# Where the lead's second-half shifts, re-roundings and gates stand in ScalarE's queue

## The chip, the cores and the metric

The kernel runs on one core of a Trainium2 chip. The metric is the device time of one execution in microseconds; the time of a kernel is the median of several runs. Beside the times there is one profiled execution, with the start and duration of each instruction on each engine: TensorE (PE, its weight loads PEld), VectorE (DVE), ScalarE (ACT), GpSimd (POOL), and SyncE (SP), which here only issues DMAs.

## The reference

One layer of a streaming encoder over 1024 positions of 1024 channels, in float32:

```python
mod = silu(c) @ w_ada + b_ada
sh1, sc1, g1, sh2, sc2, g2 = split(mod, 6)
h = rms_norm(x, norm_mix_g) * (1.0 + sc1) + sh1
proj = h @ w_in                         # 7 groups of 1024 columns
...                                     # two convolution mixers, sigmoid gates, projections
x = x + g1 * mix
h2 = rms_norm(x, norm_ffn_g) * (1.0 + sc2) + sh2
a, bgate = split(h2 @ w_ffn_in, 2)
x = x + g2 * ((silu(a) * bgate) @ w_ffn_out)
return rms_norm(x, final_norm_g)
```

The change lies in the first part: the making of `h` and the start of `h @ w_in`.

## The kernel before, in words

**Layout.** Everything is kept transposed: channels on the 128 partitions, positions along the row. A block `k` (0 to 7) is 128 channels; a half `h` (0 or 1) is 512 positions. `x[k, h]` is a tile of 128 x 512.

**Precision.** A float32 product is made of three matmuls of a rounded type: each operand is a rounded part `hi` and a rest `lo`, and `mm3` issues hi.hi, hi.lo and lo.hi. So a weight tile that has been loaded (`raw`) is cast on ScalarE (`wh`, L231) and the rest is made by a subtraction on VectorE or GpSimd (`wl`, L232); activations go the same way (`split`, L423; `t_split`, L434 and L435).

**Duals.** Most products with pairs of column blocks are done with a seven-product scheme (Strassen's; the products are named "1265734"). It needs sums and differences of quarter blocks of `h`, in float32: with b11 = `x[k, 0]`, b12 = `x[k, 1]`, b21 = `x[k + 4, 0]`, b22 = `x[k + 4, 1]` the loop at L862 makes b11 - b12, `t2`, b21's difference and, for k = 0, b22 - b12 in place, and splits `t2` for product "6".

**The lead.** While `mod` is still being made, a first stretch of columns (7 blocks of 128, `LEAD`) is computed block row by block row (`row_blocks`): for half 0 all seven, for half 1 only the three that are gates. Per block `k` of half 1, `act_x` calls `modulate`, which issues three instructions that matter here:

- VectorE: `src = src * scale * r` in place (L476);
- ScalarE: `hi` = that plus the shift, rounded (L484), and behind it VectorE's `lo` (L485);
- ScalarE: the shift added to `src` in place (L491, or L489 in half 0), which gives the float32 `h` that the sums read. In half 1 this one is not issued at once: it is put into the list `shifts`, and `act_x` takes from it two at a time, from the fifth block on, and all that is left at the eighth.

The blocks of half 1 are taken in the order `SECOND` = 5, 6, 7, 0, 1, 2, 3, 4, since the weights of 5 to 7 are still there (`kept`). `modulate.ins` holds the last call's three instructions: VectorE's first, ScalarE's `hi`, VectorE's `lo`.

After the lead the first three blocks of half 0, which had been multiplied unsplit (`WHOLE`), are re-rounded into `hi` and `lo` (`split`, L426 and L427: `h00h`, `h10h`, `h20h`); the three gate columns get their sigmoid on ScalarE (`gate`, L578) and are stored; then comes the loop of sums; then one plain column block, `gb`, with the weights `w_plain`, both halves (48 matmuls); then the duals, in the order of `win_order`: (2,"1"), (2,"2"), (0,"6"), (0,"5") and so on, each of 24 matmuls into `bank` tiles.

**Weights ahead.** `plan` is the list of weight units in the order of use. `fetch(n)` issues units (load, sums if any, cast, subtraction) until `n` are ready but unused; `next_w(ahead)` fetches `ahead + 1` and takes the first. `again_w(i)` is what the lead's second half calls for its weights.

**What sets the order.** Each engine runs its queue in order. The queues are written by a planner that goes by its own estimates of durations: an instruction listed earlier in the program comes first when both are ready, but one listed later is put ahead when an earlier one has still to wait. `with tc.issue_after(ins):` holds the instructions listed in it that run on the same engine as `ins` behind `ins`. Raw weight tiles have five buffers, `wh` and `wl` three each, so a load, a cast or a subtraction can also wait for a buffer to come free.

Of the kernel before, what the change touches and what calls it, by code (L numbers as in the profile page):

```python
# [44 lines left out]
KC = D // P  # L45
# [31 lines left out]
KEPT = 3  # L77
SECOND = [*range(KC - KEPT, KC), *range(KC - KEPT)]
# [10 lines left out]
AHEAD = 2  # L89
# [40 lines left out]
def block_kernel(ctx: ExitStack, tc: tile.TileContext, x0, xT, c, vecs, ada, w_first, w_plain, w_duals,  # L130
                 w_short, w_conf, w_o, w_fi, w_fo, w_last, outT):
    nc = tc.nc
# [36 lines left out]
    def s_tile(name, dt=F32):  # L169
        return hl_tile(name, dt)  # L170

    def g_tile(name):
        return gsp.tile([P, H], F32, tag="gs", name=name)

    def f32(t):
        return t.bitcast(F32)
# [24 lines left out]
    def modc(i):  # L201
        return mod[:, i : i + 1]
# [9 lines left out]
    def load(src, n=1024):  # L212
        raw = raw_tile(n)
        with tc.issue_after(x1_load[0]) if x1_load else ExitStack():
            load.ins = nc.sync.dma_start(raw, src).ins
        return raw
# [5 lines left out]
    def weights(src, n=1024, after=(), lo_engine=nc.vector):  # L222
        return split_w(load(src, n), n, after, lo_engine)

    def split_w(raw, n, after=(), lo_engine=nc.vector):
        wh = whp.tile([P, 1024], F32R, tag="wh", name="wh")[:, :n]
        wl = wlp.tile([P, 1024], F32R, tag="wl", name="wl")[:, :n]
        with ExitStack() as order:
            for ins in after:
                order.enter_context(tc.issue_after(ins))  # L230
            hi = nc.scalar.copy(wh, raw)  # L231
            lo = lo_engine.tensor_tensor(wl, raw, f32(wh), ALU.subtract)  # L232
        split_w.hi, split_w.lo = hi.ins, lo.ins
        if n == T and lo_engine is nc.gpsimd:
            pool_los.append((hi.ins, lo.ins))
        return wh, wl
# [101 lines left out]
        return {m: (lambda m=m: unit(m)) for m in PRODUCTS}  # L338

    plan = [None] * KC  # L340
    plan += [(w_plain[0], 1024)]
    n_duals = len(PAIRS) // 2
    win_units = [apart_units([w_duals[d, m] for m in range(4)], nc.vector, PRODUCTS if d == 0 else "125" if d == 1 else "12",
                             (lambda: t_split.ins) if d == 1 else None) for d in range(BEGUN + 1)]
# [10 lines left out]
    def next_w(ahead=AHEAD):  # L355

        fetch(ahead + 1)
        return ready.pop(0)

    def fetch(n):  # L360
        while plan and len(ready) < n:
            unit = plan.pop(0)
            ready.append(unit() if callable(unit) else weights(*unit))

    def modulation(i, raw=None):

        if raw is None:
            raw = load(ada[i])
        else:
            nc.sync.dma_start(raw, ada[i])  # L370
        modulation_of(i, raw)
# [8 lines left out]
    def affine(dst, k, sc, gains, g):  # L380
        nc.vector.scalar_tensor_tensor(
            out=dst[:, k : k + 1], in0=modc(sc + k), scalar=1.0, in1=gains[:, g + k : g + k + 1],
            op0=ALU.add, op1=ALU.mult,
        )
# [38 lines left out]

    def split(src, tile_of, name):
        hi, lo = tile_of(name + "h", dt=F32R), tile_of(name + "l", dt=F32R)
        nc.scalar.copy(hi, src)  # L426
        split.ins = nc.vector.tensor_tensor(lo, src, f32(hi), ALU.subtract).ins  # L427
        return hi, lo

# [112 lines left out]
    def squares_x(src, acc=None, clock=(), tile_of=g_tile):  # L542

        for i, t in enumerate(src):
            sq = tile_of("sq")
            act = nc.scalar.activation(sq, t, AF.Square, scale=1.0 / 32.0)
            if acc is None:
                acc = sq
            else:
                add = nc.vector.tensor_tensor(acc, acc, sq, ALU.add)  # L550
                if i in clock:
                    keep_clock(keep_clock.ins, 1, sq)
                    keep_clock(keep_clock.ins, 1, wide=True)
        squares_x.ins = act.ins, add.ins
        return acc
# [20 lines left out]
    def gate(b, j, h, ps):  # L576
        sig = g_tile("sig")
        nc.scalar.activation(sig, ps, AF.Sigmoid)  # L578
        nc.scalar.dma_start(gate_dram[b, j][:, halves[h]], sig)
# [63 lines left out]
    def first_x():  # L643

        nonlocal rx_0
        ss, r, q = rx_0
        y, t = x[0, 0], s_tile("newton")
        begin = nc.vector.scalar_tensor_tensor(out=y, in0=xin[0], scalar=naff1[:, :1], in1=r, op0=ALU.mult, op1=ALU.mult)
        nc.vector.scalar_tensor_tensor(out=t, in0=ss, scalar=EPS, in1=q, op0=ALU.add, op1=ALU.mult)
        keep_clock(keep_clock.ins, 1, t)  # L650
        keep_clock(keep_clock.ins, CLOCK[4], wide=True)
        nc.vector.scalar_tensor_tensor(out=y, in0=t, scalar=1.5, in1=y, op0=ALU.subtract, op1=ALU.mult)
        act = nc.vector.tensor_scalar(y, y, modc(0), None, ALU.add)
        with tc.issue_after(act.ins):
            begin = nc.vector.scalar_tensor_tensor(out=r, in0=t, scalar=1.5, in1=r, op0=ALU.subtract, op1=ALU.mult)
        rx_0 = r
        modulate.ins = begin.ins, act.ins, begin.ins
        return y

    def act_x(k, h=0):  # L660
        nonlocal rx_0, rx_1
        if h == 0:
            with ExitStack() as after:
                after.enter_context(tc.issue_after(squares_x.ins[1] if k in (0, X1_AT + 2) else modulate.ins[0]))
                if k == X1_AT + 2:
                    x1_load.append(act_x.last)
                    after.enter_context(tc.issue_after(x1_load[0]))
                for i in range(2 * k, 2 * k + 2):
                    modulation(i, ucp.tile([P, T + CK - 1], F32, tag="uc", name="ada")[:, :D])
            affine(naff1, k, 8, ng, V_GMIX)  # L670
            x[k, 0] = s_tile(f"x{k}0")
            if k == 0:
                return first_x()
        whole = h == 0 and k < WHOLE
        with tc.issue_after(los[-2]) if len(los) > 1 else ExitStack():
            hT[k][h] = modulate(x[k, h], rx_1 if h else rx_0, naff1[:, k : k + 1], modc(k),
                                None if whole else f"h{k}{h}", None if h else xin[k], shifts if h else None)
        if h:
            los.append(modulate.ins[2])
            for _ in range(len(shifts) if len(los) == KC else 2 * (len(los) > KEPT + 1)):  # L680
                with tc.issue_after(modulate.ins[1]):
                    shifts.pop(0)()
        if h == 0:
            if k == X1_AT:
                for i in range(KC):
                    x[i, 1] = s_tile(f"x{i}1")
                    act_x.last = nc.sync.dma_start(x[i, 1], xT[i, :, halves[1]]).ins
            elif k == X1_AT + 1:
                with tc.issue_after(modulate.ins[2]), tc.issue_after(modulate.ins[1]):
                    rx_1 = squares_x([x[i, 1] for i in range(KC)])  # L690
            elif k == X1_AT + 2:
                with tc.issue_after(modulate.ins[2]):
                    rx_1 = rstd_negative(*rx_1)
            if whole:
                return x[k, 0]
        return hT[k][h]

    los, shifts = [], []
# [10 lines left out]
    def again_w(i):  # L709

        if i < KEPT:
            return kept.pop(0)
        return next_w(1 if i < KC - 2 else AHEAD)

    rx_1 = None
    KH = KC // 2
# [128 lines left out]
    for h in range(2):  # L845
        lead = row_blocks(act_x if h == 0 else lambda i: act_x(SECOND[i], 1), GATES if h else LEAD, "lead", ops,
                          again_w if h else lead_w, 1 + h, None if h else half_way, GATES)
        if h == 0:
            ops = [(again_w(i), xs) for i, xs in ((i, act_x(SECOND[i], 1)) for i in range(3))]
        if h:  # L850
            for k in range(WHOLE):
                with tc.issue_after(modulate.ins[2]):
                    hT[k][0] = split(x[k, 0], hl_tile, f"h{k}0")
        for j, ps in enumerate(lead):
            if j < GATES:
                gate("b", j, h, ps)
            else:
                begun[(j - GATES) // 2]((j - GATES) % 2, "2", ps)


    th = {m: [None] * KH for m in PRODUCTS}
    for k in range(KH):  # L862
        (b11, b12), (b21, b22) = ((x[i, 0], x[i, 1]) for i in (k, k + KH))
        th["1"][k], th["2"][k], th["3"][k] = hT[k][0], hT[k + KH][0], hT[k + KH][1]
        nc.vector.tensor_tensor(b11, b11, b12, ALU.subtract)
        t2 = hl_tile("t2", dt=F32)
        minus(t2, b11, b22)
        minus(b21, t2, b21)
        if k == 0:
            nc.vector.tensor_tensor(b12, b22, b12, ALU.subtract)  # L870
        th["6"][k] = t_pair("t2")
        t_split(t2, *th["6"][k])
# [19 lines left out]
    b = {}  # L892
# [712 lines left out]
```

## Time and profile before

| | us |
|---|---|
| median of 3 runs | 1467.53 |
| lowest, highest | 1467.51, 1469.93 |
| the profiled execution, its own time | 1467.45 |
| its span, first to last instruction | 1465.7 |
| TensorE busy | 1452.0 |
| VectorE busy | 1183.8 |
| ScalarE busy | 623.7 |
| GpSimd busy | 503.2 |

The lead's second half is multiplied from about 60 us to 77 us of the span, `gb` from 77 to 88 us, and the duals after that. A row of the timeline reads: start in us, duration in us, engine, line of the kernel, operation, output<-inputs, shape, how many in a row, and in brackets how long the engine sat idle before it and what ended the idle time. Matmuls overlap, so the start of the next one, not the duration, tells the pace.

### The profile page before, as it was taken

How to read it: one execution, taken by the hardware profiler on the slowest of the kernel's cores; microseconds unless marked ns; L12 is line 12 of the kernel's file. 1: busy time of each engine (PE TensorE's matmuls, PEld its weight loads, DVE VectorE, ACT ScalarE, POOL GpSimd, SP SyncE). 2: the span in 40 equal slices, each digit the busy share in tenths (PEclk: the TensorE clock that was granted, in tenths of full speed). 3: DMA queues.
4: the chain of work that ended last, by engine and by line, in shares of the span. 5: the costliest groups of instructions: out<-in, count | busy, mean ns of one | idle time of the engine just before them, and what ended most of it. 6: DMA issues, size and time to landing. Idle time of an engine off the chain costs nothing.

```text
span 1465.7 us, 17764 instructions
## 1 busy us (share of the span) xinstructions
PE 1452.0 (99%) x6418; PEld 1192.1 (81%) x6418; DVE 1183.8 (81%) x1643; ACT 623.7 (43%) x911; POOL 503.2 (34%) x459
## 2 busy tenths in 40 slices
PE   9999999999999999999999999999999999999997
PEld 4778888888888888888888888888888888888887
DVE  7897999987988979999688798777777665676755
ACT  4773333333333346455225475444444343222335
POOL 0007777677677761111012002111111015435005
PEclk9999999999999999999999999999999999999999
DMA  9542232323222357486595337655454449989403
GB/s 362 194 138 85 73 101 72 115 72 101 72 87 72 130 201 273 130 256 203 198 322 187 127 116 237 222 184 189 168 173 147 146 154 368 357 279 289 138 8 115
DMA packets 85498, 251.38 MB, mean 172 GB/s; under 512 B 9841, under 2 KB 12529, under 8 KB 85410
## 3 DMA queue, kind: packets, MB, share of 16 engines
q1 hardware_dynamic: 44368, 142.04, 29.2%
q0 software_dynamic: 37008, 95.63, 19.5%
q10 hardware_dynamic: 4034, 12.59, 2.3%
q8 instruction: 50, 0.82, 0.2%
q14 instruction: 38, 0.31, 0.1%
HBM read 187.82 MB, written 62.39 MB: 171 GB/s over the span
## 4 chain that ended last, share of the span: by engine, by line
PE 88%; DVE 1%; POOL 1%; issue 1%; DMA 0%; ACT 0%; POOLq 0%; DVEq 0%
PE bank L397 11%; PE bank L395 11%; PE bank L394 11%; PE x L395 8%; PE x L397 8%; PE x L394 8%; PE z L394 4%; PE z L397 4%; PE z L395 4%; PE y L395 3%; PE y L397 3%; PE y L394 3%; PE mix L397 2%; PE mix L394 2%; PE yb L397 2%; PE yb L394 2%
## 5 line engine op out<-in xcount | busy, mean ns | idle before, releaser
L231 ACT CAST wh<-raw 128x1024 fp32r<-128x1024 f32 (+3 forms) x256 | 256.2, 1003 | 474.3 <-PE bank L395 151.4
L232 DVE TENSOR_TENSOR wl<-raw,wh 128x1024 fp32r<-128x1024 f32 (+3 forms) x177 | 203.0, 1147 | 54.1 <-ACT wh L231 52.7
L232 POOL TENSOR_TENSOR wl<-raw,wh 128x1024 fp32r<-128x1024 f32 x79 | 191.7, 2429 | 105.3 <-ACT wh L231 105.2
L969 DVE SCALAR_TENSOR_TENSOR c<-diff,vec,c 128x512 f32<-128x512 f32 x232 | 168.4, 752 | 2.7
L1319 POOL DMA_DIRECT2D hid<-stage x71 | 37.8, 533 | 344.4 <-DVE stage L435 340.3
L397 PE MATMUL bank<-th,wl 128*128 128x512 f32 x312 | 121.6, 390 | 0.5 <-POOL wl L232 0.5
L394 PE MATMUL bank<-th,wh 128*128 128x512 f32 x312 | 121.5, 389 | 0.0
L395 PE MATMUL bank<-tl,wh 128*128 128x512 f32 x312 | 121.5, 389 | 0.0
L969 DVE SCALAR_TENSOR_TENSOR c<-u,wsum,c 128x512 f32<-128x512 f32 x112 | 84.4, 753 | 2.3
L397 PEld LDWEIGHTS bank<-th,wl 128*128 128x128 f32 x312 | 58.6, 188 | 13.0 <-POOL wl L232 0.9
L394 PEld LDWEIGHTS bank<-th,wh 128*128 128x128 f32 x312 | 58.6, 188 | 12.2
L395 PEld LDWEIGHTS bank<-tl,wh 128*128 128x128 f32 x312 | 58.6, 188 | 12.1
L434 ACT CAST stage<-g 128x512 fp32r<-128x512 f32 x62 | 38.3, 622 | 63.4 <-DMA hid<-stage 42.4
L435 DVE TENSOR_TENSOR stage<-g,stage 128x512 fp32r<-128x512 f32 x62 | 42.6, 690 | 26.7 <-ACT stage L434 26.5
L309 POOL TENSOR_TENSOR raw<-raw 128x1024 f32<-128x1024 f32 x8 | 20.7, 2583 | 110.0 <-ACT th L434 104.8
L1345 POOL DMA_DIRECT2D th<-hid x71 | 38.1, 537 | 53.3 <-PE x L397 34.5
L394 PE MATMUL x<-th,wh 128*128 128x512 f32 x144 | 56.1, 389 | 0.0
L395 PE MATMUL x<-tl,wh 128*128 128x512 f32 x144 | 56.1, 389 | 0.0
L397 PE MATMUL x<-th,wl 128*128 128x512 f32 x144 | 56.1, 389 | 0.0
L395 PE MATMUL yb<-zsl,wh 128*128 128x512 f32 x128 | 49.8, 389 | 0.0
L397 PE MATMUL yb<-zsh,wl 128*128 128x512 f32 x128 | 49.8, 389 | 0.0
L394 PE MATMUL yb<-zsh,wh 128*128 128x512 f32 x128 | 49.8, 389 | 0.0
(818 smaller groups left out, 4173.7 us busy)
## 6 DMA issues: line engine op xcount, KB each, us to landing
hid<-stage POOLq DMA_DIRECT2D x71, 512.0 KB, 4.8
raw<-in_w_duals SPq DMA_DIRECT2D x57, 512.0 KB, 3.5
raw<-in_w_fi SPq DMA_DIRECT2D x54, 512.0 KB, 4.5
th<-hid POOLq DMA_DIRECT2D x71, 256.0 KB, 5.6
tl<-hid POOLq DMA_DIRECT2D x71, 256.0 KB, 5.7
ada<-in_ada SPq DMA_DIRECT2D x24, 512.0 KB, 5.3
raw<-in_ada SPq DMA_DIRECT2D x24, 512.0 KB, 4.5
raw<-in_w_fo SPq DMA_DIRECT2D x24, 384.0 KB, 5.9
```

Source lines behind the costliest of these rows:

```text
L231: hi = nc.scalar.copy(wh, raw)
L232: lo = lo_engine.tensor_tensor(wl, raw, f32(wh), ALU.subtract)
L309: unit.eng.tensor_tensor(out, x, y, ALU.add)
L394: nc.tensor.matmul(ps, wh, xh, start=first, stop=False, skip_group_check=again)
L395: nc.tensor.matmul(ps, wh, xl, start=False, stop=False, skip_group_check=again)
L397: mm3.ins = nc.tensor.matmul(ps, wl, xh, start=False, stop=last, skip_group_check=again).ins
L434: t_split.act = nc.scalar.copy(hi, src).ins
L435: t_split.ins = nc.vector.tensor_tensor(lo, src, f32(hi), ALU.subtract).ins
L969: tap.ins = nc.vector.scalar_tensor_tensor(out=out, in0=src[:, s : s + H], scalar=wt, in1=acc, op0=ALU.mult, op1=ALU.add).ins
L1319: nc.gpsimd.dma_start(hid_dram[key], s)
L1345: nc.gpsimd.dma_start(t, hid_dram[key][:, s])
```

## The change

The shifts in place of half 1 are no longer issued from `act_x`. They are issued in the loop of sums, the pair of blocks k and k + 4 directly ahead of the sums that read them, and behind the last `hi` of the lead on ScalarE. The gates of half 1 are held behind the last of the three re-roundings on ScalarE (`split.act` is recorded for that). The unit `w_plain` is a function in the plan, so that it can be held behind the last `hi` on ScalarE; `again_w` looks one unit ahead up to the seventh block and none at the eighth, where it was one up to the sixth and two from the seventh; `w_plain` is fetched after the lead by a `fetch(1)` of its own, and the unit (2,"1"), which had been fetched at the eighth block, is fetched with (2,"2") where `gb` starts, behind the sums in the listing. No instruction is added or removed.

```diff
--- before.py
+++ after.py
@@ -338,7 +338,7 @@
         return {m: (lambda m=m: unit(m)) for m in PRODUCTS}
 
     plan = [None] * KC
-    plan += [(w_plain[0], 1024)]
+    plan += [lambda: weights(w_plain[0], 1024, [modulate.ins[1]])]
     n_duals = len(PAIRS) // 2
     win_units = [apart_units([w_duals[d, m] for m in range(4)], nc.vector, PRODUCTS if d == 0 else "125" if d == 1 else "12",
                              (lambda: t_split.ins) if d == 1 else None) for d in range(BEGUN + 1)]
@@ -423,7 +423,7 @@
 
     def split(src, tile_of, name):
         hi, lo = tile_of(name + "h", dt=F32R), tile_of(name + "l", dt=F32R)
-        nc.scalar.copy(hi, src)
+        split.act = nc.scalar.copy(hi, src).ins
         split.ins = nc.vector.tensor_tensor(lo, src, f32(hi), ALU.subtract).ins
         return hi, lo
 
@@ -677,9 +677,6 @@
                                 None if whole else f"h{k}{h}", None if h else xin[k], shifts if h else None)
         if h:
             los.append(modulate.ins[2])
-            for _ in range(len(shifts) if len(los) == KC else 2 * (len(los) > KEPT + 1)):
-                with tc.issue_after(modulate.ins[1]):
-                    shifts.pop(0)()
         if h == 0:
             if k == X1_AT:
                 for i in range(KC):
@@ -710,7 +707,7 @@
 
         if i < KEPT:
             return kept.pop(0)
-        return next_w(1 if i < KC - 2 else AHEAD)
+        return next_w(1 if i < KC - 1 else 0)
 
     rx_1 = None
     KH = KC // 2
@@ -848,18 +845,23 @@
         if h == 0:
             ops = [(again_w(i), xs) for i, xs in ((i, act_x(SECOND[i], 1)) for i in range(3))]
         if h:
+            fetch(1)
             for k in range(WHOLE):
                 with tc.issue_after(modulate.ins[2]):
                     hT[k][0] = split(x[k, 0], hl_tile, f"h{k}0")
         for j, ps in enumerate(lead):
             if j < GATES:
-                gate("b", j, h, ps)
+                with tc.issue_after(split.act) if h else ExitStack():
+                    gate("b", j, h, ps)
             else:
                 begun[(j - GATES) // 2]((j - GATES) % 2, "2", ps)
 
 
     th = {m: [None] * KH for m in PRODUCTS}
     for k in range(KH):
+        with tc.issue_after(modulate.ins[1]):
+            for i in (k, k + KH):
+                shifts[SECOND.index(i)]()
         (b11, b12), (b21, b22) = ((x[i, 0], x[i, 1]) for i in (k, k + KH))
         th["1"][k], th["2"][k], th["3"][k] = hT[k][0], hT[k + KH][0], hT[k + KH][1]
         nc.vector.tensor_tensor(b11, b11, b12, ALU.subtract)
```

## The prediction

> **What bounds the kernel now.** I read the page's first part, then busy time by stage, then TensorE's waits, then the timeline around the places the diff touches.
>
> ```profile
> span 1465.7 us, 17764 instructions
> ...
> PE 1452.0 (99%) x6418; PEld 1192.1 (81%) x6418; DVE 1183.8 (81%) x1643; ACT 623.7 (43%) x911; POOL 503.2 (34%) x459
> ```
>
> TensorE is busy 99% of the span. Other engines cost time only where they make it wait. Three stages around the lead's second half (columns: PE, PEld, DVE, ACT, POOL, clock, DMA share, GB/s):
>
> ```profile
> 72.00:78.00 6.00, 5.66 (x24) 3.91 (x23) 4.85 (x7) 6.00 (x11) 0.00 (x0) 1.00 0.53 171
> 78.00:88.00 10.00, 10.00 (x45) 8.22 (x45) 10.00 (x16) 4.72 (x8) 0.00 (x0) 1.00 0.32 115
> 88.00:126.00 38.00, 38.00 (x170) 31.44 (x168) 30.18 (x37) 22.73 (x36) 14.46 (x7) 1.00 0.38 125
> ```
>
> Between 72 and 78 us ScalarE (ACT) is busy all the time and TensorE is not; from 78 us on TensorE is full and the granted clock is 1.00 in all three. The last four of TensorE's waits in the whole kernel, longest first:
>
> ```profile
> PE bank L397 <- POOL wl L232: 0.5, 1, 0.5
> PE x L395 <- DVE t4l L435: 0.5, 1, 0.5
> PE ss L561 <- DVE sq L550: 0.5, 1, 0.5
> PE lead L395 <- DVE h41l L485: 0.3, 1, 0.3
> ```
>
> Only the last is in reach: the first second-half matmul that reads `h41l`. Its size shows in TensorE's timeline:
>
> ```profile
> 72.22 0.39 PE L394 MATMUL lead<-h31h,wh 128*128 128x512 f32 x1
> ...
> 74.04 0.39 PE L397 MATMUL lead<-h31h,wl 128*128 128x512 f32 x1
> 74.35 0.96 PE L394 MATMUL lead<-h41h,wh 128*128 128x512 f32 x3
> 75.65 0.50 PE L395 MATMUL lead<-h41l,wh 128*128 128x512 f32 x1 [0.34 <-DVE h41l L485]
> ...
> 77.15 0.39 PE L394 MATMUL gb<-h00h,wh 128*128 128x512 f32 x1
> ...
> 88.14 0.39 PE L394 MATMUL bank<-h00h,wh 128*128 128x512 f32 x1
> ...
> 126.22 0.39 PE L394 MATMUL bank<-t2h,wh 128*128 128x512 f32 x1
> ```
>
> From 88.14 to 126.22 run seven products of 24 matmuls: 38.08 / 168 = 0.2267 us each, the undisturbed pace. The last 18 matmuls of the lead (two row blocks, three columns, three each) take 77.15 - 72.22 = 4.93 us instead of 18 x 0.2267 = 4.08: **0.85 us lost**. The 48 of `gb` take 10.99 instead of 10.88: another 0.11. So 0.96 us is all that this place can return, 0.07% of the time.
>
> **The change part by part.** Nothing is added or removed: the same instructions come in another order. What stands around `h41` on ScalarE and VectorE (DVE):
>
> ```profile
> 69.96 0.74 DVE L476 SCALAR_TENSOR_TENSOR x<-x,naff,rx1r 128x512 f32<-128x512 f32 x1
> ...
> 70.39 0.70 ACT L484 ACTIVATE h31h<-x,mod 128x512 fp32r<-128x512 f32 x1
> ...
> 71.00 1.32 ACT L491 ACTIVATE x<-x,mod 128x512 f32<-128x512 f32 x2
> ...
> 72.23 1.45 ACT L231 CAST wh<-raw 128x384 fp32r<-128x384 f32 x2
> ...
> 73.58 0.72 ACT L484 ACTIVATE h41h<-x,mod 128x512 fp32r<-128x512 f32 x1
> ...
> 73.71 1.23 DVE L232 TENSOR_TENSOR wl<-raw,wh 128x1024 fp32r<-128x1024 f32 x1 [0.39 <-ACT wh L231]
> ...
> 74.21 0.71 ACT L491 ACTIVATE x<-x,mod 128x512 f32<-128x512 f32 x1
> ...
> 74.82 1.03 ACT L231 CAST wh<-raw 128x1024 fp32r<-128x1024 f32 x1
> 74.85 0.75 DVE L485 SCALAR_TENSOR_TENSOR h41l<-x,mod,h41h 128x512 fp32r<-128x512 f32 x1
> 75.51 0.69 DVE L865 TENSOR_TENSOR x<-x,x 128x512 f32<-128x512 f32 x1
> ...
> 76.11 1.22 DVE L232 TENSOR_TENSOR wl<-raw,wh 128x1024 fp32r<-128x1024 f32 x1
> ...
> 76.38 0.61 ACT L426 CAST h00h<-x 128x512 fp32r<-128x512 f32 x1
> ...
> 76.89 0.58 ACT L578 ACTIVATE sig<-lead 128x512 f32<-128x512 f32 x1
> ```
>
> *The eight shifts in place* (L491). The one pair at 71.00 holds ScalarE until 72.23, 1.23 us, and two more pairs went before it. They now come behind `h41h`. Its input is ready when the DVE row of 69.96 ends at 70.70; without the pair, ScalarE has only `h31h` (to 71.00) and one cast of 384 columns (I take 0.5 of the 1.45 us that this and the 1024-column one take together) ahead of it, so `h41h` starts near 71.6, 2 us earlier. TensorE wants it at 74.27 in the present order, at 72.90 if each column's two blocks run on end. Either way it is there.
>
> *The cast and subtraction of `w_plain`* go behind `h41h`. Now the subtraction (73.71 to 74.85, 1.14 us) stands ahead of `h41l`, which could have started at 74.21: that is 0.64 of the 0.85. After, `h41l` is first, near 72.4. The weights are wanted at `gb`, which would start at 72.22 + 4.08 = 76.30. With ScalarE free at 72.3, cast 1.03 and subtraction 1.14 are done near 74.6. Worst case, with the three re-roundings (0.5 each by the starts of 76.38 and 76.89) ahead of the cast: 76.1. The subtraction's result is read in `gb`'s third matmul at the earliest, 76.75. Cost taken: 0; bounds 0 to 0.4 (the cast itself still 0.4 late if `h41h` stayed at 73.58: 73.58 + 0.63 + 1.5 + 1.0 = 76.7).
>
> *Three re-roundings, then the gates.* The gates (0.5 each) come behind `h20h`; nothing but a PSUM bank and a store hangs on them, and the store is issued behind each gate as before. Cost 0.
>
> *Shifts ahead of the sums.* Each pair's first sum L865 waits for the shifts of blocks k and k+4 in both cases. If ScalarE does all else first (three re-roundings to about 76, three gates to 77.5, the last as TensorE ends at 76.3), the first pair is done at 78.7. The row below shows that the first long step after it, `t`, runs only at 80.79 now, so this bound is not later than today:
>
> ```profile
> 80.79 0.69 DVE L439 SCALAR_TENSOR_TENSOR t<-x,x 128x512 f32<-128x512 f32 x1
> ...
> 85.01 1.23 DVE L232 TENSOR_TENSOR wl<-raw,wh 128x1024 fp32r<-128x1024 f32 x1
> ...
> 92.69 1.23 DVE L232 TENSOR_TENSOR wl<-raw,wh 128x1024 fp32r<-128x1024 f32 x1
> ```
>
> *The look-ahead* of `again_w`. The unit (2,"1"), subtracted at 76.11 now, is listed behind the sums. Ahead of it on VectorE stand at most 3 re-roundings, 4 + 4 + 4 + 1 sums and 4 subtractions, 20 of 0.60 us (the step from 75.51 to 76.11): from 74.6 to 86.6, and its own 1.14 to 87.7. TensorE wants it in the third matmul after the end of `gb`: 76.30 + 10.88 + 0.45 = 87.6. So even with no hole in VectorE's queue the cost is 0.1; with any hole (the four sums wait for ScalarE's casts in between) 0. Then (2,"2"), 1.14 us more, wanted 5.4 us later; then (0,"6"), now at 92.69 to 93.83, with two sums of 1.14 and its own: 92.3 plus a cast's 1 us. TensorE starts that product one `gb` and two products of 5.44 on, at 98.1: 5 us of cover, and if that were gone each microsecond of lateness would be one of the total.
>
> *Queues.* The loads keep their order on SP, and each waits for a raw buffer: `w_plain`'s is freed within 0.5 us of today, (2,"1")'s goes to a sum with no load. GpSimd is empty until 107.71, so nothing is passed there:
>
> ```profile
> 107.71 11.28 POOL L309 TENSOR_TENSOR raw<-raw 128x1024 f32<-128x1024 f32 x4 [104.80 <-ACT th L434]
> ```
>
> **Sum:** -0.85 in the lead, -0.11 to 0 in `gb`, +0 to +0.15 for the unit behind the sums; I take -0.8. The profiled execution took 1467.45 us (span 1465.7 and 1.75 around it): 1466.65. The median of the runs, 1467.53, is 0.08 above it: **1466.7**. What is late next is nothing here: TensorE is at its pace from `gb` to 126 us and beyond.
>
> **Rivals.**
>
> *No gain.* The stall moves from `h41l` to `gb`: if the planner leaves `h41h` at 73.58, `w_plain` is cast to 76.7 and subtracted to 77.8 as worked out above, and `gb`'s third matmul, due 76.75, is 1.05 late: -0.85 + 1.05, so 1467.2 to 1467.9. For it: ScalarE has no hole from 72 to 78. Against it: 1.23 us of shifts leaves its queue ahead of `h41h` for certain.
>
> *Slower: a unit's cast behind a gate that waits.* The cast of (2,"1") is now listed after everything that ScalarE does for the sums. Were it queued behind the two gates of `gb`, as that of (0,"6") is now,
>
> ```profile
> 88.12 0.60 ACT L578 ACTIVATE sig<-gb 128x512 f32<-128x512 f32 x1 [2.37 <-PE gb L397]
> ...
> 89.13 0.60 ACT L578 ACTIVATE sig<-gb 128x512 f32<-128x512 f32 x1
> 89.61 1.05 ACT L231 CAST wh<-raw 128x1024 fp32r<-128x1024 f32 x1
> ```
>
> then it starts 1.47 us after `gb` has ended (88.14 to 89.61): 87.2 + 1.5 + 1.0 + 1.2 = 90.9 for its subtraction, and TensorE, with two matmuls done, stands 3.2 us. Net +2.4: 1469.9, and up to 3.6 more if six of the sums are still ahead of the subtraction on VectorE: 1473.5. It decides once the stall passes 0.85 us, and is over 0.2% from 3.8. Against it: the cast is listed ahead of those gates, and its data landed long before. The Trainium skill, "TensorE: Matmul & The Clock Gate" (the table of engine queue depths), has ScalarE and VectorE as strict FIFO, which is what makes this rival possible; the trace agrees in that the cast at 89.61 stood behind the gate of 89.13.
>
> *Slower still: the clock falls in that stall.* TensorE's first matmuls show what a slow clock costs:
>
> ```profile
> 1.62 4.06 PE L587 MATMUL clock<-ones_r 128*128 128x512 f32 x10 [1.62 <-DVE ones_r L605]
> ```
>
> 0.41 us each against 0.2267. A few microseconds at that pace after a long stall add 1 to 2 us: 1471 to 1475. The same page (Part 1) says that about 3.4 us without work halves the clock and as long of work restores it, an estimated 1.7 us more; the 0.5 us stalls here left the clock at 1.00, and no row of this stage shows a longer one.
>
> *Faster by over 0.2%* would need 2.9 us, three times what the place holds; the three other stalls of 0.5 us would all have to go too.
>
> **How the numbers follow.** Full or nearly full gain 0.62, 1466.4 to 1467.1; no gain 0.18, to 1468.5 with a small new stall; the two slow rivals 0.17 together, put over 0.2%; much faster 0.03. A difference under 0.2% (2.9 us) is about what a measurement of this kernel can't tell from no change. Range: the first two cases, widened downward to the 0.96 and one more 0.5 us stall (1465.9), and upward to 1469.2 towards the slow rival.
>
> **What would show it.** In the profile after: the wait on `h41l` gone, the last 18 lead matmuls in 4.1 us, `h41h` ahead of all L491 rows and near 71.6, `w_plain`'s subtraction behind `h41l`, `gb` starting near 76.3 and the first `bank` matmul near 87.2. Wrong would be a new TensorE wait on `wl` or `wh` at the start of `gb` or of the first `bank` product, or one on `t2l` near 98.

## The result and the profile after

The changed kernel took 1474.18 us in the median of six runs (1471.95 to 1475.66), the kernel before, beside it, 1468.08 (1467.36 to 1469.93): a ratio of 1.0038, with a 95% interval of 1.0026 to 1.0051. (Ratios here and below are of the means of the runs, the times are medians.) The change made the kernel 0.4% slower, where I had forecast 0.06% faster.

The profiled execution took 1474.89 us. Its page:

```profile
span 1473.1 us, 17765 instructions
...
PE 1455.6 (99%) x6418; PEld 1193.1 (81%) x6418; DVE 1183.8 (80%) x1643; ACT 624.0 (42%) x911; POOL 503.2 (34%) x459
```

TensorE is called 99% busy as before; a loss of 7.4 us of span hardly shows in a share. The stages around the place show it (busy time of PE, PEld, DVE, ACT, POOL, then the clock, DMA share, GB/s):

```profile
72.00:78.00 6.00, 6.00 (x27) 4.62 (x26) 5.11 (x9) 5.74 (x10) 0.00 (x0) 1.00 0.53 178
78.00:88.00 10.00, 9.61 (x43) 7.64 (x42) 10.00 (x15) 8.16 (x14) 0.00 (x0) 1.00 0.21 82
88.00:98.00 10.00, 6.23 (x20) 4.62 (x21) 10.00 (x15) 6.67 (x12) 0.00 (x0) 0.83 0.52 160
88.00:126.00 38.00, 34.23 (x143) 27.84 (x144) 26.32 (x32) 20.73 (x34) 13.69 (x5) 0.96 0.39 113
```

The stage that the change aimed at, 72 to 78 us, is full now (6.00 of 6.00, 5.66 before). The ten microseconds after 88 hold 20 matmuls where the undisturbed pace has 44, and the granted clock there is 0.83. Two lines of the list of TensorE's waits (total us, times, longest us) that before did not have:

```profile
PE bank L394 <- ACT wh L231: 4.0, 2, 3.8
...
PE bank L397 <- DVE wl L232: 0.9, 2, 0.5
```

The wait on `h41l` is no longer in that list. TensorE's timeline gives the places:

```profile
71.66 0.39 PE L394 MATMUL lead<-h31h,wh 128*128 128x512 f32 x1
...
75.99 0.39 PE L394 MATMUL gb<-h00h,wh 128*128 128x512 f32 x1
...
86.86 0.39 PE L394 MATMUL bank<-h00h,wh 128*128 128x512 f32 x1
87.09 0.39 PE L395 MATMUL bank<-h00l,wh 128*128 128x512 f32 x1
87.87 0.50 PE L397 MATMUL bank<-h00h,wl 128*128 128x512 f32 x1 [0.39 <-DVE wl L232]
...
90.06 0.40 PE L397 MATMUL bank<-h30h,wl 128*128 128x512 f32 x1
94.23 0.51 PE L394 MATMUL bank<-t2h,wh 128*128 128x512 f32 x1 [3.77 <-ACT wh L231]
94.57 0.54 PE L395 MATMUL bank<-t2l,wh 128*128 128x512 f32 x1
94.91 0.63 PE L394 MATMUL bank<-h00h,wh 128*128 128x512 f32 x1
95.33 0.63 PE L395 MATMUL bank<-h00l,wh 128*128 128x512 f32 x1
...
98.21 0.39 PE L397 MATMUL bank<-h20h,wl 128*128 128x512 f32 x1
...
131.31 0.39 PE L394 MATMUL bank<-t2h,wh 128*128 128x512 f32 x1
```

The lead's last 18 matmuls take 75.99 - 71.66 = 4.33 us (4.93 before), `gb` 10.87 (10.99): 0.72 us won. Then comes a step of 0.78 instead of 0.23 at 87.87 (+0.55), one of 4.17 at 94.23 (+3.94), and behind it ten steps that take 98.21 - 94.23 = 3.98 us instead of 10 x 0.2267 (+1.71): from 94.91 to 97.89 the matmuls start 0.43 apart, about half pace. Together +5.5. The stretch from the lead's first `h31h` to the row at 131.31, which was 126.22 before, grew from 54.00 to 59.65: +5.65.

That matmul at 94.23 belongs to (0,"6"): `t2` is read by product "6" alone. It stands in TensorE's queue between the first and second columns of (2,"1"), two products ahead of its own. Before, the planner had put it there too, and it ran without a wait:

```profile
90.64 0.39 PE L397 MATMUL bank<-h30h,wl 128*128 128x512 f32 x1
90.86 0.39 PE L394 MATMUL bank<-t2h,wh 128*128 128x512 f32 x1
91.09 0.39 PE L395 MATMUL bank<-t2l,wh 128*128 128x512 f32 x1
```

What it needs is the cast of the weights of (0,"6"), which began at 89.61 before and ended 0.2 us ahead of that matmul. After, ScalarE and VectorE show:

```profile
73.96 1.22 DVE L232 TENSOR_TENSOR wl<-raw,wh 128x1024 fp32r<-128x1024 f32 x1 [0.19 <-ACT wh L231]
...
79.77 2.56 ACT L491 ACTIVATE x<-x,mod 128x512 f32<-128x512 f32 x4
...
84.23 0.72 ACT L491 ACTIVATE x<-x,mod 128x512 f32<-128x512 f32 x1
84.86 1.98 ACT L231 CAST wh<-raw 128x1024 fp32r<-128x1024 f32 x2
...
86.59 1.22 DVE L232 TENSOR_TENSOR wl<-raw,wh 128x1024 fp32r<-128x1024 f32 x1
...
91.87 1.23 DVE L309 TENSOR_TENSOR raw<-raw 128x1024 f32<-128x1024 f32 x1
...
93.13 1.04 ACT L231 CAST wh<-raw 128x1024 fp32r<-128x1024 f32 x1 [0.78 <-DVE raw L309]
```

Read it from the end: the cast starts at 93.13, when the sum of the raw weights at 91.87 is done, and that sum ran at 87.95 before. VectorE has no hole from 78 to 98 us, so the sum's place is its place in VectorE's queue, behind the subtraction of (2,"1"), which moved from 76.11 to 86.59. The cast of (2,"1") in turn stands on ScalarE behind the shifts of 79.77 and 84.23.

Not all of the loss is there. The matmul of the next norm (`mu`, at 567.67 before) starts 5.1 us later. Another 2.0 us arise between 573 and 631 us, where two short waits stand that the profile of before does not have, and 0.3 us near 1260 us; elsewhere the distance stays.

### The profile page after: what moved, and what is told of

It reads as the page before. It is cut to its first block, busy times and chain, and to the rows that moved or that the text cites. A ratio compares the mean times of both kernels' runs of the same rounds, so it can differ in the third digit from the quotient of the medians.

```text
span 1473.1 us, 17765 instructions
## 1 busy us (share of the span) xinstructions
PE 1455.6 (99%) x6418; PEld 1193.1 (81%) x6418; DVE 1183.8 (80%) x1643; ACT 624.0 (42%) x911; POOL 503.2 (34%) x459
## 4 chain that ended last, share of the span: by engine, by line
PE 86%; DVE 2%; issue 1%; POOL 1%; DMA 0%; ACT 0%; POOLq 0%; DVEq 0%
PE bank L397 11%; PE bank L394 11%; PE bank L395 10%; PE x L395 8%; PE x L397 8%; PE x L394 7%; PE z L397 4%; PE z L395 4%; PE z L394 4%; PE y L394 3%; PE y L395 3%; PE y L397 3%; PE mix L395 2%; PE yb L397 2%; PE yb L395 2%; PE mix L394 2%
```

## The experiments

In each run I also compare the stretch from the lead's first `h31h` matmul to the first `t2h` matmul near 126 us, 54.00 in before. It leaves out what differs from run to run ahead of it (that first matmul lay between 70.96 and 72.46). It is read from one profiled execution of each kernel; e3 and e11, which are the same kernel, gave 53.11 and 53.12.

| kernel | median us | ratio to before, interval | stretch us | to before's 54.00 |
|---|---|---|---|---|
| changed kernel | 1474.18 | 1.0038 (1.0026 to 1.0051) | 59.65 | +5.65 |
| e1_unit_ahead | 1470.24 | 1.0022 (1.0013 to 1.0031) | 57.42 | +3.42 |
| e2_hold_06 | 1472.41 | 1.0031 (1.0019 to 1.0043) | 58.44 | +4.44 |
| e3_look_only | 1466.11 | 0.9991 (0.9983 to 1.0000) | 53.11 | -0.89 |
| e4_shifts_only | 1470.09 | 1.0016 (1.0007 to 1.0025) | 57.74 | +3.74 |
| e5_both | 1469.57 | 1.0015 (1.0006 to 1.0024) | 55.72 | +1.72 |
| e6_filler | 1473.79 | 1.0040 (1.0026 to 1.0054) | 58.51 | +4.51 |
| e7_gates_only | 1467.60 | 1.0002 (0.9992 to 1.0011) | 54.06 | +0.06 |
| e8_before_hold | 1467.96 | 1.0001 (0.9992 to 1.0010) | 54.05 | +0.05 |
| e9_shifts_back | 1467.30 | 0.9995 (0.9986 to 1.0004) | 53.12 | -0.88 |
| e10_copies | 1466.77 | 0.9988 (0.9979 to 0.9997) | 53.40 | -0.60 |
| e11_look_again | 1466.99 | 0.9990 (0.9981 to 0.9998) | 53.12 | -0.88 |

### (2,"1") fetched early again: e1_unit_ahead

Of the changed kernel, the look-ahead alone:

```diff
         if h:
-            fetch(1)
+            fetch(2)
             for k in range(WHOLE):
```

> The changed kernel with one number changed: two units instead of one are fetched ahead of the re-roundings, so that the unit (2,"1") is listed ahead of the sums again. Theory A (the late listing of (2,"1") holds its raw buffer, which the second sum of (0,"6") needs, so that the cast of (0,"6") is late, and a matmul of (0,"6") that stands early in TensorE's queue waits for it): the subtraction of (2,"1") comes before 82 us, the cast of (0,"6") begins before 91 us, the 3.8 us wait shrinks to under 0.7 us, the clock stays, and the time is 1466.5 to 1467.5. Rival B (the shifts and gates, moved behind the lead, make ScalarE and VectorE late on their own): the wait stays near 3.8 us and the time stays 1472 or more.

The cast of (0,"6") came early again, the wait on `wl` was gone, and yet TensorE stood at the same matmul, now for another operand. ScalarE's and TensorE's timeline:

```profile
88.86 0.39 PE L397 MATMUL bank<-h30h,wl 128*128 128x512 f32 x1
...
90.17 0.62 ACT L434 CAST t2h<-t 128x512 fp32r<-128x512 f32 x1 [1.03 <-DVE t L439]
90.69 1.10 ACT L883 COPY bank<-m 128x512 f32<-128x512 f32 x2
91.33 0.50 PE L394 MATMUL bank<-t2h,wh 128*128 128x512 f32 x1 [2.08 <-ACT bank L883]
```

L883 copies a product kept from earlier into the bank that (0,"6") accumulates onto. The copies, which ran at 82.05 in the kernel before, stand behind a `t2h` cast that waits for VectorE. So the late unit was one cause, not the only one: the expected time was missed because the same matmul lost 2.24 us for its bank, and 1.7 to the clock behind it.

### The early matmul taken away: e2_hold_06

```diff
-        product(win_banks[d], m, th[m], win_evacs[d], onto="2")
+        with tc.issue_after(mm3.ins) if (d, m) == (0, "6") else ExitStack():
+            product(win_banks[d], m, th[m], win_evacs[d], onto="2")
```

> The changed kernel with the matmuls of (0,"6") held behind those of (2,"2") on TensorE; the weights are as late as in the changed kernel. Theory A: nothing in TensorE's queue waits for the late cast at 90 us any more; there remains the wait of 0.4 to 0.6 us for the subtraction of (2,"1") at 87 us; time 1466.5 to 1467.5. Rival C (the lateness alone is enough, and the wait moves to the start of (0,"6") near 98 us): 2 us or more are lost there, 1469 or more.

The time expected was missed here too. The matmuls of (0,"6") now stand behind (2,"2"), and TensorE no longer waits for that cast. But the late cast still holds ScalarE's queue, and L785, the copy that gives (2,"2") its bank, stands behind it:

```profile
93.24 0.39 PE L397 MATMUL bank<-h30h,wl 128*128 128x512 f32 x1
93.60 1.04 ACT L231 CAST wh<-raw 128x1024 fp32r<-128x1024 f32 x1 [0.77 <-DVE raw L309]
...
95.59 0.57 ACT L785 COPY bank<-bank 128x512 f32<-128x512 f32 x1
96.22 0.54 PE L394 MATMUL bank<-h40h,wh 128*128 128x512 f32 x1 [2.60 <-ACT bank L785]
```

The loss moved from (0,"6") to (2,"2"), 2.75 us instead of 3.94, and the clock fell there too. Taking the consumer out of TensorE's way does not help while the producer blocks its own queue.

### One part alone: e3_look_only, e4_shifts_only, e7_gates_only

e3 is the kernel before with the new look-ahead; the shifts stay where they were:

```diff
-        return next_w(1 if i < KC - 2 else AHEAD)
+        return next_w(1 if i < KC - 1 else 0)
...
         if h:
+            fetch(1)
             for k in range(WHOLE):
```

> The kernel before with the look-ahead edit alone (w_plain fetched behind the lead, (2,"1") listed behind the sums), shifts and gates as before. Its queue for TensorE has no matmul of (0,"6") ahead of the second column of (2,"1"). Theory A: late weights without an early matmul cost under 0.6 us, and the wait for h41l is gone since w_plain's subtraction no longer stands ahead of it: 1466.6 to 1467.8. Rival C (late listing alone is enough): 1470 or more.

e4 is the kernel before with the shifts moved and nothing else:

```diff
-            for _ in range(len(shifts) if len(los) == KC else 2 * (len(los) > KEPT + 1)):
-                with tc.issue_after(modulate.ins[1]):
-                    shifts.pop(0)()
...
     for k in range(KH):
+        with tc.issue_after(modulate.ins[1]):
+            for i in (k, k + KH):
+                shifts[SECOND.index(i)]()
```

> The kernel before with the shifts alone moved into the loop of sums; look-ahead, gates and w_plain as before. In its queue for TensorE two matmuls of (0,"6") stand even ahead of the first of (2,"1"), behind gb. Theory A (an early matmul that waits for a cast behind the gates of gb): TensorE waits 2 to 4 us at 87 us for the cast of (0,"6"), time 1468.5 to 1472. My prediction's mechanism (the move of the shifts gives 0.8 us and costs nothing): 1466.7. Rival B: slower with the wait somewhere other than on a matmul of (0,"6").

These two divide the change. e3 keeps all of the gain that I forecast (its time came out a little under the one expected): its stage behind `gb` is full,

```profile
88.00:98.00 10.00, 10.00 (x46) 8.29 (x45) 10.00 (x15) 7.37 (x13) 0.00 (x0) 1.00 0.38 107
```

with (2,"1") listed behind the sums as in the changed kernel. Two rows say why that was free:

```profile
91.14 1.05 ACT L231 CAST wh<-raw 128x1024 fp32r<-128x1024 f32 x1
...
97.85 0.39 PE L394 MATMUL bank<-t2h,wh 128*128 128x512 f32 x1
```

The cast of (0,"6") is late here as well, at 91.14 against 89.61 before; but in e3's queue for TensorE no matmul of that product stands between the columns of (2,"1"), and its first one comes at 97.85. (The same holds for e9 below: cast at 91.46, first matmul at 98.19.) So e3 shows that late weights cost nothing when no early matmul waits for them, and not that they are harmless beside one.

In e4, (0,"6") even came ahead of (2,"1"), directly behind `gb`, while its cast stood behind both gates of `gb`:

```profile
86.24 0.39 PE L397 MATMUL gb<-h71h,wl 128*128 128x512 f32 x1
87.44 0.60 ACT L578 ACTIVATE sig<-gb 128x512 f32<-128x512 f32 x1
87.93 1.04 ACT L231 CAST wh<-raw 128x1024 fp32r<-128x1024 f32 x1
89.03 0.79 PE L394 MATMUL bank<-t2h,wh 128*128 128x512 f32 x1 [2.40 <-ACT wh L231]
89.62 0.63 PE L395 MATMUL bank<-t2l,wh 128*128 128x512 f32 x1
```

The step from 86.24 to 89.03 loses 2.56 us, and the eight steps behind it 1.6 more, most of them at half pace. The cast itself is not late in e4: it begins 16.9 us after the lead's first `h31h`, and 17.4 us after it in before. It is the matmul that stands earlier. So the moved shifts cost by themselves, here by the place that the planner then gives a matmul; the late listing of the unit costs nothing by itself. e7 is the kernel before with the gates held behind the last re-rounding:

```diff
-        nc.scalar.copy(hi, src)
+        split.act = nc.scalar.copy(hi, src).ins
...
-                gate("b", j, h, ps)
+                with tc.issue_after(split.act) if h else ExitStack():
+                    gate("b", j, h, ps)
```

> The kernel before with one part alone: the second-half gates held behind the re-rounding of h20. My prediction's cost for it: 0, with no new wait on TensorE between 70 and 126 us; the wait for h41l stays. 1467 to 1468. Rival B (gates late cost on their own, by PSUM banks that come free later): a new wait of 1 us or more, 1469 or more.

It changed neither the time nor the 0.3 us wait for `h41l`.

### Both cures, and a filler: e5_both, e6_filler

e5 takes e1's and e2's edits together.

> The changed kernel with both edits: (2,"1") listed ahead of the sums and the matmuls of (0,"6") held behind those of (2,"2"). Theory A': each of the two alone left one wait (with the unit ahead, the early matmul of (0,"6") waited 2.1 us for the copy into its bank, L883; with the matmul held, the copy L785 that (2,"2") needs stood in ScalarE's queue behind the late cast). With both, no wait over 0.6 us is left between 70 and 126 us and the clock there stays at 1.00: 1465.5 to 1467. Rival B (moving shifts and gates costs on its own): 1468.5 or more, with a new wait on ScalarE's work.

The expected 1465.5 to 1467 was missed, and what the text there calls rival B came: TensorE waited once more for L785, which now stood behind the two copies L883 and three casts:

```profile
91.72 1.11 ACT L883 COPY bank<-m 128x512 f32<-128x512 f32 x2
92.58 0.39 PE L397 MATMUL bank<-h30h,wl 128*128 128x512 f32 x1
92.76 1.65 ACT L434 CAST th<-x 128x512 fp32r<-128x512 f32 x3
94.32 0.57 ACT L785 COPY bank<-bank 128x512 f32<-128x512 f32 x1
...
94.95 0.50 PE L394 MATMUL bank<-h40h,wh 128*128 128x512 f32 x1 [1.98 <-ACT bank L785]
95.28 0.39 PE L395 MATMUL bank<-h40l,wh 128*128 128x512 f32 x1
```

2.14 us are lost, and here the clock stayed at 1.00: the next matmuls start 0.33 and then 0.23 apart. e6 is e2 with small matmuls on constants put into TensorE's queue ahead of (2,"2"); nothing reads what they make:

```diff
-        product(win_banks[d], m, th[m], win_evacs[d], onto="2")
+        if (d, m) == (2, "2"):
+            keep_clock(mm3.ins, 20)
+        with tc.issue_after(keep_clock.ins) if (d, m) in ((2, "2"), (0, "6")) else ExitStack():
+            with tc.issue_after(mm3.ins) if (d, m) == (0, "6") else ExitStack():
+                product(win_banks[d], m, th[m], win_evacs[d], onto="2")
```

> The kernel with (0,"6") held and weights late (time 1472.4, one wait of 2.6 us ahead of (2,"2")), with 20 small matmuls of a constant put into that wait, some 2 us of work whose result nobody reads. If the clock falls because TensorE idles there: the wait that is left is under 0.8 us, the first ten matmuls of (2,"2") start 0.23 us apart instead of 0.43, granted clock 1.00 from 88 to 126 us, and the time is 1.5 to 2.2 us shorter, 1470 to 1471. If the clock has no part: matmuls stay 0.43 apart or the time stays 1472 to 1473.

```profile
92.34 4.63 PE L587 MATMUL clock<-ones 128*128 128x128 f32 x40
96.72 0.48 PE L394 MATMUL bank<-h40h,wh 128*128 128x512 f32 x1
97.04 0.39 PE L395 MATMUL bank<-h40l,wh 128*128 128x512 f32 x1
```

The filler took 96.72 - 92.34 = 4.38 us (the 20 matmuls stand as 40 in the trace), where some 2 us were meant, and more than the 2.75 us hole that it was to fill. So the time got no better, and the expected one was missed. It did show that the slow matmuls come from TensorE's idleness: with the hole filled, the next ones start 0.23 to 0.32 apart and the clock stays at 1.00.

### Undoing: e8_before_hold, e9_shifts_back

e8 puts e2's hold into the kernel before; e9 is the changed kernel with the shifts taken back into `act_x` (the reverse of e4's diff).

> The kernel before with the matmuls of (0,"6") held behind those of (2,"2"), nothing else; ScalarE's and VectorE's queues up to 105 us stand as before. Theory A: the early matmuls cost nothing in the kernel before, because their cast was done 0.3 us ahead of them; same time, 1467 to 1468. If holding them gave 1 us or more (1466.5 or less), the early order would have had a price of its own.

> The changed kernel with the shifts alone put back to where they were (issued from act_x, two at a time); look-ahead, w_plain's hold and the gates' hold stay changed. Theory D (the move of the shifts is what costs: it leaves ScalarE's later casts and copies, and with them an early matmul of (0,"6"), late for TensorE): no wait over 0.6 us between 70 and 126 us, and the time is that of the look-ahead alone, 1465.5 to 1467. If the late listing of (2,"1") were the cause: 1470 or more.

e8: no difference, so the early matmuls of (0,"6") cost nothing as long as their cast is in time. e9: the loss is gone and the lead's gain is there:

```profile
88.00:98.00 10.00, 10.00 (x46) 8.29 (x45) 10.00 (x15) 7.69 (x13) 0.00 (x0) 1.00 0.19 73
```

Its stretch is that of e3, 53.12. With the shifts back, the planner also put the first matmul of (0,"6") at 98.19, so e9 takes away the early matmul together with the moved shifts. Its median is not told from before's: its profile has waits near 612 us, of the kind that the changed kernel has at 619.

### The remaining copies moved: e10_copies, and e3 again: e11_look_again

If with the shifts moved it is only ScalarE's copies that come in the wrong order, then e5 with the two L883 copies listed where (0,"6") is listed should lose nothing:

```diff
-    for p in range(2):
-        nc.scalar.copy(win_banks[0]["x", p], m1[p])
...
+        if (d, m) == (0, "6"):
+            for p in range(2):
+                nc.scalar.copy(win_banks[0]["x", p], m1[p])
```

> The kernel with the unit ahead and (0,"6") held, where TensorE still waited 2.0 us ahead of (2,"2") for the copy L785, with one more edit: the two copies of m1 (L883) are listed ahead of (0,"6") instead of ahead of the duals, so that L785 comes directly behind the last cast of t2 on ScalarE. The shifts stay moved. Theory D with the place of the price as read (ScalarE's queue order between the last t2 cast and L785): the wait is under 0.5 us and the time 1465.5 to 1467.3. If the moved shifts cost elsewhere too: another wait takes its place and the time stays over 1468.5.

> The kernel before with the look-ahead edit alone, a second time on the same chip as the other two. If it is a gain: ratio under 1.000 with its interval, near 0.999, 1465.5 to 1467. If its first ratio was chance: 1.000 within its interval.

```profile
90.09 0.62 ACT L434 CAST t2h<-t 128x512 fp32r<-128x512 f32 x1 [1.03 <-DVE t L439]
90.61 0.58 ACT L785 COPY bank<-bank 128x512 f32<-128x512 f32 x1
...
91.70 0.39 PE L394 MATMUL bank<-h40h,wh 128*128 128x512 f32 x1
```

L785 comes directly behind the `t2h` cast and is done 0.5 us before TensorE wants its bank. TensorE's list shows no wait between 70 and 126 us, with the shifts still moved. At 1466.77 us it is 0.1% faster than before, as is e3 when run again, at 1466.99; the two are not told apart. So the shifts' place costs next to nothing directly: it costs through the order in which the planner then writes the queues, of ScalarE's casts and copies (e1, e2, e5) and of TensorE's matmuls (e4).

## Why the prediction was wrong

**The lead.** Right. `h41h` was to start near 71.6 and started at 72.26, since the VectorE step that it waits for (L476) began at 71.48 and not at 69.96; the wait on `h41l` is gone; the last 18 matmuls were to take 4.1 us and took 4.33, in e3 4.09. Of the 0.85 us e3 and e9 return all, with the shifts where they were; the shifts alone (e4) return 0.41, at 4.52. So the whole gain can be had from `w_plain`'s place behind `h41l`, and the move that cost the time was not needed for it.

**`gb`, the gates, `w_plain`.** Right: `w_plain` was to be ready between 74.6 and 76.1, and its subtraction ran from 73.96 to 75.1; `gb` was to start near 76.3 and did at 75.99; the gates cost 0 (e7).

**(2,"1") behind the sums.** VectorE's subtraction was worked out for 86.6 to 87.7 and came at 86.59, in part by luck: of the 20 steps of 0.60 us that the sum put ahead of it only 15 stood there, and in place of the other five two sums of weights (80.11 and 81.85, 1.14 each) that it had not counted there; and the row began at 75.10 instead of 74.6. The price was to be 0 to 0.15 and was 0.55: in this run TensorE came to the lead 0.56 us sooner than in the profile of before, while VectorE's end did not move with it. The term was a difference of two absolute times with no margin.

**(0,"6").** This is the step that failed. The text says "TensorE starts that product one `gb` and two products of 5.44 on, at 98.1: 5 us of cover". It took the order of the products for the order of TensorE's queue. The queue held the first matmuls of that product between the columns of (2,"1"), at 90.86 in the profile of before, so the cover of its cast was 0.2 us, not 5; and the bound that the same sentence gives, "if that were gone each microsecond of lateness would be one of the total", is what was paid: 3.94 us of waiting, and 1.71 of slow matmuls on top. The prediction's own figures would have shown more than half of the wait. Its chain for VectorE starts the cast near 87.7 + 1.14 + 2 x 1.14 = 91.1 and ends it near 92.2, and the early matmul was due at 87.2 + (90.86 - 88.14) = 89.9. The cast then came at 93.13, since the sum of its weights stood behind steps of the sums that the chain had put ahead of (2,"1"). I had the row of the cast (89.61) in the text and did not ask what its end released. That the shifts' new place would move casts and copies behind them on ScalarE I did not ask either: they were priced only by when the sums could start.

**The rivals.** The slow ones had the right kind: a unit's cast late in ScalarE's queue, and the clock falling in that stall. They named the wrong unit, (2,"1") for (0,"6"), and the wrong place; their 1471 to 1475 holds the measured 1474.18, in part by chance, as some 2 us of the loss arose elsewhere, between 573 and 631 us. The weight of 0.17 was set by looking at that one unit. The clock's term, "1 to 2 us", measured 1.71. The 1.7 estimated there from the Trainium skill, "TensorE: Matmul & The Clock Gate" (Part 1), agrees with it; its 3.4 us without work as what halves the clock does not (last section).

**Open.** The 2.0 us between 573 and 631 us. Waits of 0.3 to 0.5 us near 612 to 620 us appear in e2, e9 and e11 too, and not in e3, which is the same kernel as e11: that part varies between executions. It is no explanation of the 6 us, since e3, e9 and e11 are not slower, but I cannot say how much of the last 2 us belongs to the change. Nor do the runs show by which of its estimates the planner orders the queues of ScalarE and TensorE as it does; and no run has late weights with an early matmul and the shifts in their old place.

## What to carry to other kernels

When a listing is changed in front of a planner, work out the cover of each operand that comes later from the place where the engine's own queue wants it, not from the order of the products: look in the timeline for matmuls of a later product among those of an earlier one, and for each cast and copy that releases them. Price a moved instruction by what then stands behind it on its own engine, too. A change of several edits is cheap to divide: the look-ahead alone is 0.1% faster, the shifts alone 0.16% slower.

## What was not expected of the hardware

TensorE's clock fell after short holes. The steps that lost 2.24 us (e1), 2.56 (e4) and 2.75 (e2) were each followed by six to eight steps of 0.43 us instead of 0.23, with a granted clock of 0.83 over ten microseconds in e1 and e4, and cost 1.6 to 1.7 us beside the wait; the step that lost 2.14 us (e5) was not. The Trainium skill, "TensorE: Matmul & The Clock Gate" (Part 1), gives about 3.4 us of idleness as what halves the clock; here less was enough, and the measurement decides.

The traces also record the moment at which the granted clock changes. In the four kernels in which it fell, it fell 26 (changed kernel), 25 (e1), 26 (e2) and 24 (e4) times 3.413 us after the first entry of that record, near the kernel's start, and was back at 1.00 after 3.413 us more. So the time falls into fixed steps of that length, and the row below is of the step at whose end the clock fell, or, for e5, of the step with most of the hole:

| kernel | step, us of the span | TensorE without work in it, us | clock in the next step |
|---|---|---|---|
| changed kernel | 91.25 to 94.66 | 2.98 | 0.50 |
| e2_hold_06 | 93.13 to 96.54 | 2.60 | 0.50 |
| e4_shifts_only | 85.39 to 88.81 | 2.18 | 0.50 |
| e1_unit_ahead | 88.57 to 91.98 | 2.08 | 0.50 |
| e5_both | 93.17 to 96.58 | 1.78 | 1.00 |

In e1 the fall came 0.65 us after the hole had ended (91.33), in e4 0.22 us ahead of its end (89.03): it is the end of a step that sets the moment, not the end of the hole. In e5 the end of a step, at 93.17, cut the hole in two, with 0.20 us in the step ahead. The same section of that page has the chip look at windows of fixed length that a kernel's start does not reset, so that the moment of a change shifts from run to run; these steps agree with it. All five rows fit a bound between 1.78 and 2.08 us without work in one step. Whether a hole as long as e5's would halve the clock if it lay in one step, no run here shows.
